# A hybrid streaming encoder layer: convolution sums moved to PSUM, part of the weight splitting moved to GpSimd

## The chip, the core and the metric

The kernel runs on one core of a Trainium2 chip. The metric is the device time of one execution in microseconds (us); the median of several runs is taken. TensorE (PE in the profile) does the matrix products, VectorE (DVE) and ScalarE (ACT) the work on elements, GpSimd (POOL) a few small copies, and SyncE (SP) issues all transfers.

## What is computed

One layer with three branches, fed by one projection of the normed input, for 512 prompt tokens and 64 sample tokens, 1024 channels wide (some steps left out):

```python
h = _rmsnorm(x, norm_pre_w)
proj = h @ w_in
glu_v, glu_g, conv_gate, z, xbc, dt_raw, q, xa_gate, gates = jnp.split(proj, points, axis=-1)

u = glu_v * jax.nn.sigmoid(glu_g)
c, new_a = _causal_dwconv(u, st_a, conv_dw_w, conv_dw_b)      # width 31
c = jax.nn.silu(_layernorm(c, conv_ln_w, conv_ln_b)) * jax.nn.silu(conv_gate)
out_a = c @ conv_out_w

xbc_c, new_ssd = _causal_dwconv(xbc, st_ssd, ssd_conv_w, ssd_conv_b)   # width 4
...                                       # state-space scan, gating, grouped norm
out_b = y.astype(x.dtype) @ ssd_out_w

s = jnp.einsum('bthd,bmhd->bhtm', qh, mem_k) * (XA_HEAD_DIM ** -0.5)
p = jax.nn.softmax(s, axis=-1)
o = jnp.einsum('bhtm,bmhd->bthd', p, mem_v)
out_c = (o * jax.nn.silu(xa_gate)) @ xa_out_w

g = jax.nn.sigmoid(gates + gate_b).reshape(bsz, t, N_BRANCH, D_MODEL)
m = g[:, :, 0] * out_a + g[:, :, 1] * out_b + g[:, :, 2] * out_c
x_new = x + _rmsnorm(m @ w_out, norm_post_w)
```

Cross-attention has 4 heads of 256 over 256 memory tokens. The long convolution, of width 31, is the one whose sums the change moves.

## The kernel before

**Tiling.** Channels lie on the 128 partitions and the 576 tokens along the free axis. Every projection is a job: one 1024 x 128 block of weights (or 512 x 256), loaded as a `raw` tile of 128 x 1024. Each float is split in two: ACT rounds it to a high part `whi` (L183), and the difference `raw - whi` is the low part `wlo` (L184, on DVE). The activations are split likewise (`hT[0]`, `hT[1]`, or `split`), and three products are summed for each of 8 blocks of rows: high by high, high by low, low by high (`mac`, L204). Two halves of 288 tokens make 48 matmuls for a whole projection. There are 153 jobs in a list `order`, and one of them ("dt") has no tile of its own for the low part; `prep_to` makes the parts of a job when the job two places ahead of it is asked for, and `raw`, `whi` and `wlo` have 3 buffers each.

**Stages.** First norm and transposes, then four groups of the state-space branch (to about 470 us in the profile) with their projections; in and after the last of them the gates of the long convolution (`glu(j)`, two projections gg and gv for each of the 8 channel blocks). Then the merge gate of the second branch (g1), the attention heads (for each head: key, query, key, query, two value jobs, two output gates xg; in heads 1 to 3 also a `glu`), the merges of the third branch (g2, oc), the gate cg of the convolution branch, its layer norm, and the merges of the first branch (g0, oa). At the end `out_rows` multiplies by w_out: four row blocks for each half of the channels, and `out_sample` after the second row block of the second half.

**The long convolution.** `conv_ops(j)` makes 32 operations for a channel block: a start value by ACT (L762: first tap and bias), 30 taps by DVE (L769: `c = u shifted * weight + c`, 606 columns), and the sum over blocks `csum` (L776, L778). They go in a list `bg`, and `bgrun(n)` puts n of them between the projections. `push_conv` takes two blocks at a time and lets them alternate: a tap of one, a tap of the other. The sums `c` lie in SBUF, a pool of 8 tiles (`c8`), from the first tap to the layer norm, which uses them as `cact[j]`.

**PSUM.** Two pools from start to end: `pmm` with 2 tiles of 2 x 512 columns for projections ("mm" in the profile), and `pps` with 4 tiles of 512 columns for everything else ("ps": transposes, key and value projections, attention scores, outputs of the heads, rows of the last product).

**Order.** The code states an order, but each engine's order is made when the kernel is built, `TileContext(nc, schedule_with_timeline_sim=True)`: an operation takes its place by its turn in the code, when its operands and a buffer are to be had. `keep_in_program_order` holds an operation (all taps, among others) to the order of the code, and `bgrun` runs with a lower turn. Once built, each engine works through its own list strictly in order.

**GpSimd's own work** after 376 us: for each `glu` a zero fill and a copy of the sample's state in `u` (L727, L728), and two small copies of the ends of `u` (L731, L732), which wait for DVE.

Of the kernel before, what the change touches and what calls it, by code (L numbers as in the profile page):

```python
# [8 lines left out]
F32 = mybir.dt.float32  # L9
F32R = mybir.dt.float32r  # L10
AF = mybir.ActivationFunctionType
ALU = mybir.AluOpType
# [16 lines left out]
def hybrid_trunk_kernel(  # L29
# [9 lines left out]
    nc = tc.nc  # L39
    PSUM = bass.MemoryType.PSUM  # L40
# [5 lines left out]
    wp = ctx.enter_context(tc.tile_pool(name="wp", bufs=2))  # L46
    big = ctx.enter_context(tc.tile_pool(name="big", bufs=1))
    pmm = ctx.enter_context(tc.tile_pool(name="pmm", bufs=2, space=PSUM))
    pps = ctx.enter_context(tc.tile_pool(name="pps", bufs=4, space=PSUM))
    dram = ctx.enter_context(tc.tile_pool(name="dram", bufs=1, space=bass.MemoryType.DRAM))  # L50

    def mm_tile():
        return pmm.tile([128, 2, 512], F32, tag="mm", name="mm")

    def ps_tile():
        return pps.tile([128, 512], F32, tag="ps", name="ps")


    ident = const.tile([128, 128], F32, name="ident")
# [102 lines left out]
    pos = {o[0]: i for i, o in enumerate(order)}  # L162
    ready = {}
    nprep = [0]

    def prep_to(n):
        while nprep[0] <= min(n, len(order) - 1):
            name, src, c0, r0, kk, cols = order[nprep[0]]
            raw = wp.tile([128, 1024], F32, tag="raw", name="raw", bufs=3)
            hi = wp.tile([128, 1024], F32R, tag="whi", name="whi", bufs=3)  # L170
            lo = wp.tile([128, 1024], F32R, tag="wlo", name="wlo", bufs=3) if name != "dt" else hi
            n_ = kk * cols
            nc.sync.dma_start(
                out=raw[:, :n_].rearrange("p (k c) -> p k c", k=kk),
                in_=src[r0:r0 + 128 * kk, c0:c0 + cols].rearrange("(k p) c -> p k c", p=128),
            )
            if name == "dt":
                w = hi[:, :2 * n_].rearrange("p (k c) -> p k c", k=kk)
                rw, wh, wl = raw[:, :n_].rearrange("p (k c) -> p k c", k=kk), w[:, :, 0:32], w[:, :, 32:64]
                a = nc.scalar.activation(wh, rw, AF.Copy)  # L180
                b = nc.vector.tensor_tensor(wl, rw, wh.bitcast(F32), ALU.subtract)
            else:
                a = nc.scalar.activation(hi[:, :n_], raw[:, :n_], AF.Copy)  # L183
                b = nc.vector.tensor_tensor(lo[:, :n_], raw[:, :n_], hi[:, :n_].bitcast(F32), ALU.subtract)  # L184
            if nprep[0] in (2, 3):
                tc.keep_in_program_order(a)
                tc.keep_in_program_order(b)
            ready[name] = (w, None) if name == "dt" else (
                hi[:, :n_].rearrange("p (k c) -> p k c", k=kk),
                lo[:, :n_].rearrange("p (k c) -> p k c", k=kk),  # L190
            )
            nprep[0] += 1

    def W(name):
        i = pos[name]
        prep_to(i + LA)
        return ready.pop(name)
# [46 lines left out]
    for t in range(5):  # L244
        n = 128 if t < 4 else 64
        if t < 4:
            x_t = obf[:, D * t:D * t + D]
        else:
            x_t = s2.tile([128, D], F32, tag="M", name="x4")
        nc.sync.dma_start(out=x_t[:n], in_=xp_d[128 * t:128 * t + 128] if t < 4 else xs_d)  # L250
        xt.append((x_t, n))
        if t == 0:
            wpre = s2.tile([128, D], F32, tag="R", name="wpre")
            nc.sync.dma_start(out=wpre, in_=norm_pre_w[0].partition_broadcast(128))
        if t == 1:
            prep_to(1)
# [11 lines left out]
    def x_tr(t):  # L268
        x_t, n = xt[t]
        rms_tile(x_t, n, sqx, ssx[:, t], wpre)  # L270
        for b in range(2):
            p = ps_tile()
            for k in range(4):
                kc = 512 * b + 128 * k
                m = nc.tensor.transpose(p[:, n * k:n * k + n], x_t[:n, kc:kc + 128], ident[:n, :n])
                tc.keep_in_program_order(m)
            v = p[:, :4 * n].rearrange("p (k t) -> p k t", k=4)
            d = slice(128 * t, 128 * t + n)
            nc.scalar.activation(hT[0][:, 4 * b:4 * b + 4, d], v, AF.Copy)
            nc.vector.tensor_tensor(  # L280
                hT[1][:, 4 * b:4 * b + 4, d], v, hT[0][:, 4 * b:4 * b + 4, d].bitcast(F32), ALU.subtract
            )

    def warm_pe(n):
        p = ps_tile()
        for _ in range(n):
            tc.keep_in_program_order(nc.tensor.matmul(p[:, 0:128], lhsT=ident, rhs=ident, start=True, stop=True))
# [27 lines left out]
    def tr_act(tiles, k, dst, wcol, ncols):  # L315
        pt = ps_tile()
        c = 0
        for x_t, n in tiles:
            nc.tensor.transpose(pt[:, c:c + n], x_t[:n, 128 * k:128 * k + 128], ident[:n, :n])
            c += n  # L320
        nc.scalar.activation(dst[0][:, k, :], pt[:, :ncols], AF.Copy, scale=vecs[:, wcol + k:wcol + k + 1])
        nc.vector.scalar_tensor_tensor(
            dst[1][:, k, :], pt[:, :ncols], vecs[:, wcol + k:wcol + k + 1],
            dst[0][:, k, :].bitcast(F32), ALU.mult, ALU.subtract,
        )
# [323 lines left out]
    def out_b(g, q):  # L649
        w = W(f"ob{g}_{q}")  # L650
        act = ([a for a, _ in yhl[g]], [b for _, b in yhl[g]])
        for i in range(2):
            m = 2 * q + i
            pt = proj(w, act=act, c0=128 * i)
            if g == 0:
                nc.scalar.activation(v2(ob[:, m]), va(pt), AF.Copy)
            else:
                nc.vector.tensor_tensor(v2(ob[:, m]), v2(ob[:, m]), va(pt), ALU.add)  # L658
# [13 lines left out]
    upad, cact = {}, {}  # L672
    bg = []
# [66 lines left out]
    for q in range(4):  # L740
        out_b(3, q)
    st.close()

    st = ExitStack()
    c8 = st.enter_context(tc.tile_pool(name="c8", bufs=8, reuse_waits="tile"))
    NC = 606
# [7 lines left out]
    def conv_ops(j):  # L754
        w31 = dww.rearrange("p (r j) -> p r j", r=31)
        box = []

        def first():
            c = c8.tile([128, NC], F32, tag="c", name="c")
            box.append(c)  # L760
            cact[j] = c
            nc.scalar.activation(  # L762
                c, upad[j][:, 0:NC], AF.Identity, scale=w31[:, 0, j:j + 1], bias=vecs[:, V_DWB + j:V_DWB + j + 1]
            )

        def tap(r):
            c = box[0]
            tc.keep_in_program_order(
                nc.vector.scalar_tensor_tensor(  # L769
                    c, upad[j][:, r:r + NC], w31[:, r, j:j + 1], c, ALU.mult, ALU.add  # L770
                )
            )

        def add():
            if j == 0:
                nc.vector.tensor_copy(csum, box[0])  # L776
            else:
                nc.vector.tensor_tensor(csum, csum, box[0], ALU.add)  # L778

        return [first] + [lambda r=r: tap(r) for r in range(1, 31)] + [add]  # L780

    def push_conv(*js):
        for ops in zip(*[conv_ops(j) for j in js]):
            bg.extend(ops)

    push_conv(0, 1)
    memT = [memp.tile([128, KD, NMEM], F32R, name=f"memT{i}") for i in range(2)]
    mt_ = []
# [6 lines left out]
    glu(3, sx, "xs", 7)  # L795
    glu(4, sx, "xs", 7)
    push_conv(2, 3)


# [90 lines left out]
    for h in range(4):  # L890
# [4 lines left out]
        cv = a1.tile([128, 2, 256], F32, tag="cv", name="cv")  # L895
# [20 lines left out]
        for tp in range(3):  # L916
            ps = ps_tile()
# [29 lines left out]
        for i in range(2):  # L947
            j = 2 * h + i
# [11 lines left out]
        if h > 0:  # L960
            glu(4 + h, sx, "xs", 7)
            if h != 2:
                push_conv(3 + h, 4 + h)
# [77 lines left out]
    for j in range(8):  # L1041
        c = cact[j]
# [111 lines left out]
    st3.close()  # L1154
    st.close()
    stx.close()


_INS = [
# [32 lines left out]
```

## Time and profile before

| | |
|---|---|
| median of 3 runs | 1123.3 us (1122.68 to 1123.66) |
| profiled execution | 1122.15 us |
| its span, first to last instruction | 1120.4 us |
| mean granted TensorE clock | 0.999 |
| GpSimd busy | 56.8 us in 146 instructions |
| long convolution's taps on DVE | 240, from 504.7 to 890.4 us |
| low parts on DVE | 152, from 10.7 to 1043.0 us |

How to read the rows: a row of the groups gives line, engine, operation, out<-in, shapes and count, then busy time and mean duration in ns, then the idle time of the engine before them and what ended it. A row of the timeline gives start, duration, engine, line, operation and count; rows of several instructions are merged. A row of the windows gives a stretch, and for PE, PEld, DVE, ACT, POOL the busy time and, in brackets, the instructions, then granted clock, share of the DMA engines and GB/s. A row of the waits gives who waited for whom, the total, the number and the longest. A row of the chain of waits gives start, duration and what ran. In the answer for one line, three numbers with slashes are the shortest, median and longest duration in ns.

### The profile page before, as it was taken

To read this page: it belongs to the slowest core of one execution; us is meant where nothing else is said; L and a number is where in the kernel's file an instruction comes from. 1 tells how busy PE (TensorE), PEld (TensorE's weight loads), DVE (VectorE), ACT (ScalarE), POOL (GpSimd) and SP (SyncE) were. 2 spreads that over 40 slices of the span, in tenths; PEclk is the share of its full clock that TensorE was granted. 3 is DMA by queue.
4 is the path that set the end of the run, shared out by engine and by line. 5 is a ranking of instruction groups with operands and counts; after the bars stand their busy time and mean duration, and the time that the engine had idled before them with its cause. 6 is when DMAs were issued, how large, how long until landed. Compare 5 with 4: busy or idle time off the path is not lost.

```text
span 1120.4 us, 20083 instructions
## 1 busy us (share of the span) xinstructions
PE 1109.5 (99%) x8285; PEld 1070.9 (96%) x8285; DVE 829.1 (74%) x1268; ACT 481.9 (43%) x844; POOL 56.8 (5%) x146
## 2 busy tenths in 40 slices
PE   8999999999999999999999999999999999999997
PEld 8999999999999999999999999999999999999974
DVE  5778897578868885756899996998588868714533
ACT  5564664456436442543224453434421245522331
POOL 0100110011002100100000000000000000000000
PEclk9999999999999999999999999999999999999999
DMA  7354423442353232242445343434353234233502
GB/s 208 95 162 122 143 82 94 129 117 81 97 144 107 83 81 78 75 124 76 135 139 142 85 131 95 123 85 116 84 160 93 76 84 106 76 94 104 178 20 85
DMA packets 183233, 120.74 MB, mean 108 GB/s; under 512 B 12422, under 2 KB 173230, under 8 KB 183142
## 3 DMA queue, kind: packets, MB, share of 16 engines
q1 hardware_dynamic: 183142, 119.46, 37.4%
q8 instruction: 65, 1.06, 0.4%
q14 instruction: 26, 0.21, 0.1%
HBM read 110.13 MB, written 9.31 MB: 107 GB/s over the span
## 4 chain that ended last, share of the span: by engine, by line
PE 97%; DMA 1%; ACT 1%; SPq 0%; DVE 0%; issue 0%; DVEq 0%; ACTq 0%
PE mm L204 78%; PE ps L204 4%; PE ps L887 2%; PE ps L886 2%; PE ps L888 2%; PE ps L561 2%; PE ps L587 2%; PE ps L565 1%; DMA ob<-in_x_prompt_dram 1%; PE ps L526 1%; PE ps L1130 1%; PE ps L518 1%; PE mm L346 0%; DMA out_dram<-ho 0%; PE ps L483 0%; PE ps L937 0%
## 5 line engine op out<-in xcount | busy, mean ns | idle before, releaser
L204 PE MATMUL mm<-hT,whi 128*128 128x288 f32 (+2 forms) x3328 | 588.3, 297 | 0.8 <-DVE hT L280 0.3
L204 PEld LDWEIGHTS mm<-hT,whi 128*128 128x128 f32 x3328 | 495.1, 189 | 3.6 <-issue 1.3
L204 PE MATMUL mm<-hT,wlo 128*128 128x288 f32 (+2 forms) x1664 | 363.9, 297 | 0.0
L183 ACT ACTIVATE whi<-raw 128x1024 fp32r<-128x1024 f32 x152 | 160.9, 1059 | 401.0 <-PE mm L204 323.9
L204 PEld LDWEIGHTS mm<-hT,wlo 128*128 128x128 f32 x1664 | 273.6, 189 | 1.1 <-issue 0.7
L184 DVE TENSOR_TENSOR wlo<-raw,whi 128x1024 fp32r<-128x1024 f32 x152 | 185.8, 1222 | 116.0 <-ACT whi L183 115.7
L769 DVE SCALAR_TENSOR_TENSOR c<-u,dww,c 128x606 f32<-128x606 f32 x240 | 191.5, 844 | 0.0
L204 PE MATMUL mm<-hi,whi 128*128 128x288 f32 x512 | 111.4, 298 | 0.0
L204 PE MATMUL mm<-lo,whi 128*128 128x288 f32 x512 | 110.9, 296 | 0.0
L204 PE MATMUL mm<-hi,wlo 128*128 128x288 f32 x512 | 110.4, 296 | 0.0
L204 PEld LDWEIGHTS mm<-hi,whi 128*128 128x128 f32 x512 | 82.2, 189 | 0.9 <-issue 0.9
L204 PEld LDWEIGHTS mm<-hi,wlo 128*128 128x128 f32 x512 | 82.5, 188 | 0.2 <-issue 0.2
L204 PEld LDWEIGHTS mm<-lo,whi 128*128 128x128 f32 x512 | 82.5, 188 | 0.0
L454 DVE SCALAR_TENSOR_TENSOR acc<-xp,scw,acc 128x579 f32<-128x579 f32 x72 | 58.4, 815 | 3.1 <-ACT acc L450 1.9
L658 DVE TENSOR_TENSOR ob<-ob,mm 128x576 f32<-128x576 f32 x24 | 18.0, 750 | 16.3 <-PE mm L204 16.2
L547 ACT ACTIVATE M<-R,tok 128x128 f32<-128x128 f32 (+1 forms) x80 | 24.8, 379 | 12.3 <-PE ps L587 12.3
L446 POOL COPY tails<-xp 128x3 f32<-128x3 f32 x24 | 18.0, 751 | 193.2 <-ACT xp L444 187.9
L887 PE MATMUL ps<-lo,hi 128*128 128x512 f32 x64 | 25.3, 397 | 0.0
L888 PE MATMUL ps<-hi,lo 128*128 128x512 f32 x64 | 25.1, 395 | 0.0
L886 PE MATMUL ps<-hi 128*128 128x512 f32 x64 | 24.9, 397 | 0.0
L565 PEld LDWEIGHTS ps<-bc,h 128*128 128x128 f32 x128 | 16.5, 191 | 8.8 <-issue 6.6
L204 PE MATMUL ps<-whi,memT 128*128 128x256 f32 x128 | 23.5, 282 | 0.0
(292 smaller groups left out, 1287.8 us busy)
## 6 DMA issues: line engine op xcount, KB each, us to landing
raw<-in_w_in_dram SPq DMA_DIRECT2D x104, 512.0 KB
R<-scr SPq DMA_DIRECT2D x16, 512.0 KB
raw<-in_ssd_out_w_dram SPq DMA_DIRECT2D x16, 512.0 KB
raw<-in_xa_kv_w_dram SPq DMA_DIRECT2D x16, 512.0 KB
raw<-in_xa_out_w_dram SPq DMA_DIRECT2D x8, 512.0 KB
raw<-in_conv_out_w_dram SPq DMA_DIRECT2D x8, 512.0 KB
wraw<-in_w_out_dram SPq DMA_DIRECT2D x8, 512.0 KB
E<-scr SPq DMA_DIRECT2D x24, 128.0 KB
```

Of the source, the lines that this page charges most:

```text
L183: a = nc.scalar.activation(hi[:, :n_], raw[:, :n_], AF.Copy)
L184: b = nc.vector.tensor_tensor(lo[:, :n_], raw[:, :n_], hi[:, :n_].bitcast(F32), ALU.subtract)
L204: m = nc.tensor.matmul(o, lhsT=w, rhs=r[:, s:s + w_], start=(i == 0 and a == 0), stop=(i == n - 1 and a == 2),)
L454: nc.vector.scalar_tensor_tensor(acc, xp[:, r:r + 579], w4[:, r, jt:jt + 1], acc, ALU.mult, ALU.add)
L547: nc.scalar.activation(M[:, 4 + e, :], R[:nl, 4 + e, :], AF.Relu, scale=-1.0, bias=tok[:nl, 0, c, a + 4:a + 5])
L561: nc.tensor.matmul(pS, lhsT=bt[:nl], rhs=xw[:nl], start=True, stop=True)
L565: nc.tensor.matmul(po[:, nl * j:nl * j + nl], lhsT=h[:, 128 * j:128 * j + 128], rhs=gC[g][:, cs], start=True, stop=True,)
L587: nc.tensor.matmul(pd[o:o + 64, nl * (e // 2):nl * (e // 2) + nl], lhsT=xd[:nl, 64 * e:64 * e + 64], rhs=M[:, e, :], start=True, stop=True,)
L769: nc.vector.scalar_tensor_tensor(c, upad[j][:, r:r + NC], w31[:, r, j:j + 1], c, ALU.mult, ALU.add)
L886: nc.tensor.matmul(out, lhsT=wh, rhs=rh, start=(i == 0), stop=False)
L887: nc.tensor.matmul(out, lhsT=wh, rhs=rl, start=False, stop=False)
L888: nc.tensor.matmul(out, lhsT=wl, rhs=rh, start=False, stop=(i == n - 1))
```

## The change

Three things. The convolution's sum is built in a PSUM tile of 1024 columns, of which 606 are used, in a pool with a single buffer; when a channel block is complete, ACT copies it to the SBUF tile that the layer norm uses, and DVE adds it to `csum` from PSUM. `push_conv` puts the blocks one after the other. To make room, the pool of 4 `ps` tiles is closed after the state-space branch and the last `out_b`, and a pool of 2 takes its place until the end. And for jobs behind `gv2` in the list, every second (odd place) has its low part made by GpSimd instead of DVE.

```diff
-    pps = ctx.enter_context(tc.tile_pool(name="pps", bufs=4, space=PSUM))
+    stp = ExitStack()
+    pps = stp.enter_context(tc.tile_pool(name="pps", bufs=4, space=PSUM))
...
+    psp = [pps]
+
     def ps_tile():
-        return pps.tile([128, 512], F32, tag="ps", name="ps")
+        return psp[0].tile([128, 512], F32, tag="ps", name="ps")
...
                 a = nc.scalar.activation(hi[:, :n_], raw[:, :n_], AF.Copy)
-                b = nc.vector.tensor_tensor(lo[:, :n_], raw[:, :n_], hi[:, :n_].bitcast(F32), ALU.subtract)
+                eng = nc.gpsimd if nprep[0] > pos["gv2"] and nprep[0] % 2 else nc.vector
+                b = eng.tensor_tensor(lo[:, :n_], raw[:, :n_], hi[:, :n_].bitcast(F32), ALU.subtract)
...
     st.close()
+    stp.close()
+    stp = ExitStack()
+    pcv = stp.enter_context(tc.tile_pool(name="pcv", bufs=1, space=PSUM))
+    psp[0] = stp.enter_context(tc.tile_pool(name="pps2", bufs=2, space=PSUM))
...
         def first():
-            c = c8.tile([128, NC], F32, tag="c", name="c")
+            c = pcv.tile([128, 1024], F32, tag="cv", name="cacc")[:, 0:NC]
             box.append(c)
-            cact[j] = c
...
         def add():
+            cact[j] = c8.tile([128, NC], F32, tag="c", name="c")
+            nc.scalar.activation(cact[j], box[0], AF.Copy)
             if j == 0:
                 nc.vector.tensor_copy(csum, box[0])
...
     def push_conv(*js):
-        for ops in zip(*[conv_ops(j) for j in js]):
-            bg.extend(ops)
+        for j in js:
+            bg.extend(conv_ops(j))
...
     stx.close()
+    stp.close()
```

## The prediction

> **What bounds the kernel now.** I read the page first, then the windows by stage, TensorE's own waits, and the timeline at the places that the change touches.
>
> ```profile
> span 1120.4 us, 20083 instructions
> ...
> PE 1109.5 (99%) x8285; PEld 1070.9 (96%) x8285; DVE 829.1 (74%) x1268; ACT 481.9 (43%) x844; POOL 56.8 (5%) x146
> ...
> DVE  5778897578868885756899996998588868714533
> ...
> PE 97%; DMA 1%; ACT 1%; SPq 0%; DVE 0%; issue 0%; DVEq 0%; ACTq 0%
> ```
>
> ```profile
> 0.00:15.00 15.00, 12.04 (x73) 11.25 (x73) 7.04 (x10) 9.69 (x18) 1.89 (x16) 1.00 0.95 271
> 15.00:476.00 461.00, 460.09 (x3554) 440.07 (x3555) 360.75 (x621) 241.08 (x458) 44.24 (x108) 1.00 0.37 106
> 476.00:1036.00 560.00, 560.00 (x4250) 556.92 (x4249) 425.02 (x582) 208.03 (x324) 10.66 (x22) 1.00 0.38 107
> 1036.00:1120.40 84.40, 77.35 (x412) 62.65 (x410) 36.28 (x59) 23.09 (x46) 0.00 (x0) 0.98 0.29 94
> ```
>
> TensorE (PE) is busy 1109.5 of 1120.4 us and is 97% of the chain that ended last. A busy PE could still be a slow one, so I check the rate and the waits.
>
> ```profile
> 655.00 12.80 PE mm L204 x96
> ```
>
> ```profile
> PE ps L287 <- POOL dtb L327: 1.6, 1, 1.6
> PE ps L1139 <- ACT ysq L1136: 0.8, 1, 0.8
> ```
>
> In the chain two whole projections of 48 matmuls take 12.80 us, 0.133 us for each of 288 columns, without a gap; the granted clock is 1.00 in that stage. The largest waits of PE are 1.6 us at the start and 0.8 us at the end. The change acts from the third gate projection on (about 476 us). From there to 1036 us PE is busy in all of the 560.00 us, while VectorE (DVE) has 560 - 425 = 135 us to spare and GpSimd (POOL) works for 10.7. So **a microsecond taken from DVE is worth nothing here, and a microsecond in which PE waits is added to the end.** What could be gained is the 7.05 us without PE work after 1036; most of it is the last row's evacuation and store, which the change leaves alone, and the rest is the 0.8 us above. A difference of 0.2%, 2.2 us, is about what a measurement of this kernel can tell from no change.
>
> **The change, part by part.**
>
> *Low parts on GpSimd.* After the third gate projection, jobs with an odd place in the list make their low part on GpSimd: 47 of 152 (counted in the list).
>
> ```profile
> L184 DVE TENSOR_TENSOR wlo<-raw,whi 128x1024 fp32r<-128x1024 f32 x152 | 185.8, 1222 | 116.0 <-ACT whi L183 115.7
> ...
> L769 DVE SCALAR_TENSOR_TENSOR c<-u,dww,c 128x606 f32<-128x606 f32 x240 | 191.5, 844 | 0.0
> ```
>
> DVE loses 47 x 1.222 = 57 us; none of it lies on PE's path: worth 0. What matters is whether a low part on GpSimd is late. The tightest of those 47 jobs that I found, the second key job of a head:
>
> ```profile
> 685.39 1.06 ACT L183 ACTIVATE whi<-raw 128x1024 fp32r<-128x1024 f32 x1 [8.19 <-PE mm L204]
> ```
>
> ```profile
> 694.69 0.40 PE L204 MATMUL ps<-memT,whi 128*128 128x256 f32 x2
> ```
>
> Its high part is ready at 686.45 and its first matmul runs at 694.69: 8.2 us of cover. (The second value job of a head has less, but its place is even and it stays on DVE.) No row shows a GpSimd operation of this size with two inputs.
>
> ```profile
> L237 POOL CAST onesr<-mask 128x128 fp32r<-128x128 f32 x1 | 0.3, 298 | 0.0
> ```
>
> ```profile
> L446 POOL COPY tails<-xp x24: 188/762/2412, 29.2 to 368.1; 128x3 f32<-128x3 f32 x24
> ```
>
> ```profile
> 136.20 1.22 DVE L184 TENSOR_TENSOR wlo<-raw,whi 128x1024 fp32r<-128x1024 f32 x1
> ```
>
> ```profile
> 136.27 1.20 POOL L446 COPY tails<-xp 128x3 f32<-128x3 f32 x1 [8.53 <-ACT xp L444]
> ```
>
> Bounds: below, DVE's own 1.22 us; above, the one-input cast of 128 columns times 8, and twice for two inputs, 4.8 us, plus the worst blocking: the tiny copy of L446 takes 0.19 us at best and 2.41 at worst, 2.2 more. That makes 7.0 us, still under 8.2. I take the cast times 8 and the copies' median blocking, 2.4 + 0.6 = 3.0 us. Cost on the path: 0, hidden by the two projections that run between a weight's making and its use. The raw buffer comes free up to 6 us later, and with it the next weight load on SP's queue and what stands behind it; the buffers run three jobs ahead, so 0 too. On POOL's own queue the low parts stand between the gates' small copies, which wait for DVE (L731 for L729); such a wait must also stay under 8.2 us.
>
> The row at 136.27 shows the copy ending with the DVE operation that has two SBUF inputs. The Trainium skill ("SBUF — State Buffer", Who interferes with whom) says that these two kinds block each other, the later one for the whole of the earlier. The trace agrees for GpSimd waiting; no row here shows DVE waiting, which is a rival below.
>
> *Sums in PSUM.* The 240 taps now read and write a PSUM tile. No row has a DVE write to PSUM; reading it costs nothing extra (L534 reads PSUM, L1050 does not, both 512 wide):
>
> ```profile
> L534 DVE TENSOR_TENSOR xd<-ps,tok 128x512 f32<-128x512 f32 x16 | 10.9, 680 | 0.0
> ...
> L1048 DVE SCALAR_TENSOR_TENSOR c<-th,c 128x606 f32<-128x606 f32 x8 | 6.0, 784 | 0.0
> ...
> L1050 DVE TENSOR_TENSOR hi<-hi,c 128x512 f32<-128x512 f32 x8 | 5.5, 685 | 0.0
> ...
> L1017 ACT ACTIVATE lsq<-c 128x606 f32<-128x606 f32 x7 | 4.9, 709 | 3.7 <-DVE csum L1018 3.7
> ```
>
> One tile at a time also means that each tap follows the one it depends on, where two channel blocks alternated before.
>
> ```profile
> 127.61 2.53 DVE L454 SCALAR_TENSOR_TENSOR acc<-xp,scw,acc 128x579 f32<-128x579 f32 x3
> ```
>
> ```profile
> 639.21 2.37 DVE L769 SCALAR_TENSOR_TENSOR c<-u,dww,c 128x606 f32<-128x606 f32 x3
> ```
>
> Three dependent operations of L454 (815 ns each) start (2.53 - 0.815)/2 = 0.857 us apart, 0.042 more than one lasts; three alternating taps (2.37 - 0.844)/2 = 0.763 apart, 0.081 less. So up to 0.12 us a tap, 240 x 0.12 = 29 us of DVE; in PSUM I take the same, with +-14 us as bounds (0.06 a tap, the gap between 844 and the 784 of L1048, a tap's width without the per-channel scalar). DVE still ends with 14 us or more fewer, inside its 135 spare: 0 on the path. Each block adds an ACT copy of 0.7 us (L1017's width); its tile is single, so between blocks the taps pause for that copy and the next start value, some 2 us seven times, with other DVE work to do. Cost: 0.
>
> *Half of the small PSUM tiles.* The new PSUM tile takes the room of two of the four [128, 512] tiles ("ps") from the opening of the new pools to the end. This is where PE can wait, and the only part that I give a price. In heads 1 to 3 three ps tiles are live when the value projection starts:
>
> ```profile
> 644.79 0.60 PE L860 MATMUL ps<-ident,kf 128*128 128x128 f32 x4
> 645.23 0.60 PE L911 MATMUL ps<-ident,ck 128*128 128x128 f32 x4
> 645.58 0.36 PE L204 MATMUL ps<-whi,memT 128*128 128x256 f32 x1
> ```
>
> ```profile
> 644.72 1.07 ACT L183 ACTIVATE whi<-raw 128x1024 fp32r<-128x1024 f32 x1 [1.93 <-PE mm L204]
> ...
> 646.22 0.59 ACT L862 ACTIVATE kk<-ps 128x512 f32<-128x512 f32 x1
> ```
>
> ```profile
> 645.86 1.22 DVE L184 TENSOR_TENSOR wlo<-raw,whi 128x1024 fp32r<-128x1024 f32 x1
> 647.00 0.75 DVE L904 TENSOR_TENSOR qlo<-mm,qhi 128x576 fp32r<-128x576 f32 x1
> ```
>
> With two, the matmul at 645.58 waits until ACT has copied the keys out, 646.22 + 0.59 = 646.81: 1.23 us. Head 3:
>
> ```profile
> 763.74 0.37 PE L204 MATMUL ps<-whi,memT 128*128 128x256 f32 x1
> ```
>
> ```profile
> 764.38 0.59 ACT L862 ACTIVATE kk<-ps 128x512 f32<-128x512 f32 x1
> ```
>
> Again 764.97 - 763.74 = 1.23; three heads 3.7 us. If PE fills each gap with the first four matmuls of the next projection, whose high part is ready at 645.79 (4 x 0.133 = 0.53; the fifth needs the low part), 2.1 remain. I take 2.1, bounds 0 and 3.7.
>
> Head 0 has no gate projections after it to fill with:
>
> ```profile
> 632.28 0.55 PE L956 MATMUL ps<-pts,cv 128*128 128x64 f32 x4
> 632.64 0.48 PE L204 MATMUL ps<-memT,whi 128*128 128x256 f32 x2
> ```
>
> ```profile
> 633.37 0.68 DVE L953 SCALAR_TENSOR_TENSOR oc<-ps,xs 128x512 f32<-128x512 f32 x1
> ...
> 634.72 0.68 DVE L953 SCALAR_TENSOR_TENSOR oc<-ps,xs 128x512 f32<-128x512 f32 x1
> ```
>
> Both tiles then hold results that DVE takes out until 634.05 and 635.40; the next key projection moves from 632.64 to 635.40, 2.8 us. If DVE comes to them earlier by a tap and a query split (0.84 + 0.75, the latter from L904) it is 1.2. I take 2.0. In the other heads 13 us of gate matmuls are there to fill: 0.
>
> At the end two tiles suffice for the rows, since one row is taken out while the next one's 24 matmuls run; only after the sample rows both tiles are held until DVE's L1137:
>
> ```profile
> 1102.50 0.69 DVE L1137 TENSOR_TENSOR y<-ps,x4r 128x512 f32<-128x512 f32 x1 [3.89 <-ACT ysq L1136]
> ```
>
> ```profile
> 1102.77 0.48 PE L886 MATMUL ps<-hi 128*128 128x512 f32 x1
> ```
>
> 1103.19 - 1102.77 = 0.4 us.
>
> **Sum:** 2.1 + 2.0 + 0.4 = 4.5 us. The profiled execution took 1122.15 us (span 1120.4), so 1126.65; it lies 1.15 under the median of the three runs, 1123.3, which gives **1127.8**.
>
> **The rivals.**
>
> *PE is refilled; no loss* (the other side: not slower). The order on PE is made anew and other matmuls move into each gap. Place: the value projections and head 0's end. For it: in the rows above PE already starts tiles out of the order of the code whenever one is missing, and never waits in 560 us. Against: at 645.58 the next projection's low part comes only at 647.08 (L184 at 645.86 + 1.22), and in the changed kernel GpSimd makes it (its place is odd). It decides from the point where each gap has more than 1.2 us of ready matmuls. Price 0: 1123.3, or 1122.5 with the 0.8 us wait gone too.
>
> *DVE blocked by GpSimd, tiles late.* If a GpSimd low part blocks DVE's operations as DVE blocked the copy at 136.27, a low part made by DVE waits up to 3.0 us, and behind it in DVE's order the maxima and the evacuations of ps (L871, L941, L953). With four tiles that was hidden; with two, one such delay in each head reaches PE: 4 x 3.0 = 12 us more, 1139.8. Against it: some 45 low parts, and those are spread over 550 us, so that most meet no such neighbour. By the Trainium skill's rule above, the taps, left with one tensor in SBUF, would not be blocked.
>
> *Low parts too late.* Over 8.2 us, each further microsecond costs 47 us: at 8.5, 1138 to 1142. It needs more than my upper bound of 7.0.
>
> *Faster by more than 2.2 us.* Nothing but shorter matmuls could do it, and none is touched.
>
> **How the numbers follow.** Forecast (1125.6 to 1131) 0.45; refilled 0.34; DVE blocked 0.14; low parts too late 0.03; faster 0.04. All unknowns at their lower ends give 1122.5, all PE waits at their upper ends 3.7 + 2.8 + 0.4 = 6.9, 1130.2. Range 1122.4 to 1137: it leaves out the faster case and the upper half of the blocked one, and what lies past it. Both signs of cases hold much of the chance, so the likeliest one's own range, 1125.6 to 1131, stands beside it. Faster 0.04; same 0.35; slower 0.61.
>
> **What would show it.** Right: PE busy falls short of the stage 476 to 1036 by some 4 us, TensorE's waits list ACT L862 and DVE L953, DVE is down 15 to 60 us, and the end moves by what PE waits. Wrong: PE gains waits on GpSimd's L184 (low parts late), or on DVE operations that last 2 us or more (blocking), or none at all (refilled). A change in the matmuls' 0.133 us would void the whole argument.

## The result and the profile after

| | before | after |
|---|---|---|
| median | 1122.99 us (4 runs, 1122.50 to 1123.66) | 1131.72 us (4 runs, 1130.24 to 1132.12) |
| ratio, 95% interval | | 1.0075 [1.0057, 1.0092] |
| profiled execution | 1122.15 us | 1132.04 us |

The changed kernel is slower by 8.7 us, 0.75%. First the page of the kernel after: the span, the busy times, and from the costliest groups the taps and the low parts made by GpSimd.

```profile
span 1130.3 us, 20124 instructions
...
PE 1112.8 (98%) x8285; PEld 1071.7 (95%) x8285; DVE 825.4 (73%) x1221; ACT 487.4 (43%) x852; POOL 168.5 (15%) x193
...
L776 DVE SCALAR_TENSOR_TENSOR cacc<-u,dww,cacc 128x606 f32<-128x606 f32 x240 | 203.9, 850 | 9.8 <-ACT cacc L769 4.9
...
L188 POOL TENSOR_TENSOR wlo<-raw,whi 128x1024 fp32r<-128x1024 f32 x47 | 116.5, 2479 | 412.0 <-ACT whi L186 310.3
```

DVE lost 47 low parts of 1.22 us, 57 us, and yet is busy only 3.7 us less (829.1 to 825.4). Something gave nearly all of it back. The window of the kernel after for the stage used before (columns as there):

```profile
476.00:1036.00 560.00, 554.96 (x4183) 549.52 (x4183) 418.63 (x532) 210.44 (x328) 116.45 (x67) 1.00 0.37 104
```

Where PE was busy in all of 560 us it now lacks 5.04. Of TensorE's waits in the kernel after, these three are new behind 476 us:

```profile
PE mm L208 <- DVE hi L468: 3.2, 1, 3.2
PE ps L208 <- ACT kk L871: 1.7, 4, 1.0
...
PE ps L895 <- ACT sss L1149: 0.4, 1, 0.4
```

There is one of 3.2 us for the evacuation of a gate cg (`hi`, the product after the tanh, L464 before and L468 now), four for the copy of the keys `kk`, and 0.4 at the tail. The largest was not in the forecast's sum. Here is its place, the layer norm, in the timeline of the kernel after:

```profile
938.45 2.40 POOL L188 TENSOR_TENSOR wlo<-raw,whi 128x1024 fp32r<-128x1024 f32 x1 [9.86 <-ACT whi L186]
...
939.06 7.33 DVE L1052 TENSOR_TENSOR c<-c,mean 128x606 f32<-128x606 f32 x8
...
946.32 0.74 DVE L468 SCALAR_TENSOR_TENSOR hi<-hi,mm 128x576 f32<-128x576 f32 x1
...
947.12 0.80 PE L208 MATMUL mm<-hT,whi 128*128 128x288 f32 x4 [3.17 <-DVE hi L468]
...
948.14 1.17 PE L208 MATMUL mm<-hT,whi 128*128 128x288 f32 x4
...
949.58 1.17 PE L208 MATMUL mm<-hT,whi 128*128 128x288 f32 x4
```

and the same place in the timeline of the kernel before:

```profile
936.00 0.74 DVE L464 SCALAR_TENSOR_TENSOR hi<-hi,mm 128x576 f32<-128x576 f32 x1
936.65 5.68 DVE L1043 TENSOR_TENSOR c<-c,mean 128x606 f32<-128x606 f32 x8
...
944.40 0.75 DVE L464 SCALAR_TENSOR_TENSOR hi<-hi,mm 128x576 f32<-128x576 f32 x1
```

The reader is to see three things. The eight products with the tile `mean` (which by then holds the reciprocal deviation) take 7.33 us in place of 5.68, and they begin while GpSimd makes a low part; one of them lasts 2.43 us and the other seven 0.77. The evacuation that PE needs stands behind these eight in DVE's list; before, one stood ahead of them. And after the wait PE comes back slowly: from 948.14 to 949.58 it starts six matmuls (two lie between the rows), one in 0.24 us where 0.133 was the rule. The window behind the wait, of the kernel after, shows how long (the column before the last two is the granted clock):

```profile
947.00:951.00 4.00, 3.88 (x18) 3.89 (x19) 4.00 (x7) 0.33 (x1) 0.00 (x0) 0.61 0.37 85
951.00:955.00 4.00, 4.00 (x31) 4.00 (x31) 4.00 (x9) 2.50 (x4) 0.00 (x0) 0.97 0.39 116
```

The clock lacks 0.39 of 4 us and 0.03 of 4 us, 1.7 us together, as half a clock for 3.4 us would give. In 3.4 us at 0.24 a matmul PE starts 14 of them, which would have taken 1.9: 1.5 us is lost on top of the 3.2. In this execution one evacuation that came late cost 4.7 us; what the clock adds differs from one execution to the next, as the last section shows.

Which operations of DVE got longer is in its groups, kernel after and then kernel before (count | busy us, mean ns of one | idle before):

```profile
L1001 DVE TENSOR_TENSOR ob<-ob,xs 128x576 f32<-128x576 f32 x8 | 15.3, 1918 | 0.1
...
L1021 DVE TENSOR_TENSOR c<-c,mean 128x606 f32<-128x606 f32 x8 | 7.9, 1050 | 0.0
...
L1052 DVE TENSOR_TENSOR c<-c,mean 128x606 f32<-128x606 f32 x8 | 7.3, 982 | 0.0
```

```profile
L992 DVE TENSOR_TENSOR ob<-ob,xs 128x576 f32<-128x576 f32 x8 | 6.0, 753 | 0.0
...
L1012 DVE TENSOR_TENSOR c<-c,mean 128x606 f32<-128x606 f32 x8 | 5.7, 783 | 0.0
L1043 DVE TENSOR_TENSOR c<-c,mean 128x606 f32<-128x606 f32 x8 | 5.7, 784 | 0.0
```

All of these read two tensors in SBUF. The taps, which now read one in SBUF and one in PSUM, keep their time (844 to 850). So the first theory was that **GpSimd's low parts stop DVE where it reads two SBUF tensors**, which costs nothing in most places and some 5 us at the layer norm; the two `ps` tiles cost the rest. Against it stood two rivals: that the sums, now complete later (the last tap starts at 895.51 and not at about 890.4), push the layer norm into the gates; and that the two tiles upset everything.

### The profile page after: what moved, and what is told of

Same layout as the page of the kernel before. It is cut to its first block, busy times and chain, and to the rows that moved or that the text cites. A ratio compares the mean times of both kernels' runs of the same rounds, so it can differ in the third digit from the quotient of the medians.

```text
span 1130.3 us, 20124 instructions
## 1 busy us (share of the span) xinstructions
PE 1112.8 (98%) x8285; PEld 1071.7 (95%) x8285; DVE 825.4 (73%) x1221; ACT 487.4 (43%) x852; POOL 168.5 (15%) x193
## 5 line engine op out<-in xcount | busy, mean ns | idle before, releaser
L776 DVE SCALAR_TENSOR_TENSOR cacc<-u,dww,cacc 128x606 f32<-128x606 f32 x240 | 203.9, 850 | 9.8 <-ACT cacc L769 4.9
L188 DVE TENSOR_TENSOR wlo<-raw,whi 128x1024 fp32r<-128x1024 f32 x105 | 128.1, 1220 | 95.3 <-ACT whi L186 94.7
L188 POOL TENSOR_TENSOR wlo<-raw,whi 128x1024 fp32r<-128x1024 f32 x47 | 116.5, 2479 | 412.0 <-ACT whi L186 310.3
L1000 DVE SCALAR_TENSOR_TENSOR lo<-lo,mm 128x576 f32<-128x576 f32 x8 | 6.0, 754 | 27.1 <-PE mm L208 27.1
```

The source lines that it names most:

```text
L188: b = eng.tensor_tensor(lo[:, :n_], raw[:, :n_], hi[:, :n_].bitcast(F32), ALU.subtract)
L776: nc.vector.scalar_tensor_tensor(c, upad[j][:, r:r + NC], w31[:, r, j:j + 1], c, ALU.mult, ALU.add)
```

## The experiments

Each kernel was timed together with the kernel before. The table gives medians and the ratio to the kernel before; 0.1% is 1.1 us. "Sums" says where the convolution's sum is built.

| kernel | low parts on GpSimd | sums | ps tiles | median us | ratio [95%] |
|---|---|---|---|---|---|
| the change | 47 | PSUM | 2 | 1131.72 | 1.0075 [1.0057, 1.0092] |
| e1 | 47 | SBUF | 4 | 1141.42 | 1.0159 [1.0146, 1.0173] |
| e2 | none | PSUM | 2 | 1126.23 | 1.0034 [1.0021, 1.0046] |
| e3 | none | SBUF | 2 | 1127.30 | 1.0039 [1.0027, 1.0052] |
| e4 | 42, none at the norm | PSUM | 2 | 1126.23 | 1.0029 [1.0018, 1.0041] |
| e5 | 47, mean in PSUM | PSUM | 2 | 1127.60 | 1.0041 [1.0028, 1.0053] |
| e6 | 5, at the norm only | SBUF | 4 | 1128.48 | 1.0046 [1.0032, 1.0060] |
| e7 | none | SBUF, one tile at a time | 4 | 1123.00 | 1.0003 [0.9994, 1.0012] |
| e8 | 42, none at the norm | SBUF | 4 | 1135.62 | 1.0111 [1.0097, 1.0124] |
| e9 | 42, none at the norm | PSUM | 2, values in mm | 1123.20 | 1.0005 [0.9997, 1.0014] |
| e10 | none | SBUF | 2, values in mm | 1123.02 | 1.0004 [0.9995, 1.0013] |

### e1: the low parts on GpSimd alone

On the kernel before:

```diff
-                b = nc.vector.tensor_tensor(lo[:, :n_], raw[:, :n_], hi[:, :n_].bitcast(F32), ALU.subtract)
+                eng = nc.gpsimd if nprep[0] > pos["gv2"] and nprep[0] % 2 else nc.vector
+                b = eng.tensor_tensor(lo[:, :n_], raw[:, :n_], hi[:, :n_].bitcast(F32), ALU.subtract)
```

> The kernel before, with only the 47 low parts on GpSimd: four ps tiles, sums in SBUF, two blocks alternating. Theory 'DVE blocked at the layer norm': the low parts on GpSimd stretch DVE's additions and products with two SBUF inputs (0.70 us each before) to 2 us and more where both run, the evacuation of a gate cg comes late, and TensorE loses some 5 us there (3.2 of wait, 1.7 of a halved clock). This kernel then shows nearly all of that: 1123.0 + 5 = 1128, with PE waits on the evacuation of mm and none on the keys' copy kk. Rival 'the sums are late': the later last tap of the sums moves the layer norm; this kernel keeps the old sums, so 1123.0 and no new wait of PE. Rival 'two small tiles': also 1123.0.

Measured: 1141.42 us, 18.6 over the kernel before, over twice the whole change. Every theory missed this; the sign of the first was right and its size far too small. TensorE's waits in e1:

```profile
PE ps L889 <- DVE qlo L905: 3.3, 3, 2.1
PE mm L205 <- DVE hi L465: 3.2, 1, 3.2
PE ps L888 <- DVE ptl L942: 2.4, 2, 1.2
PE ps L205 <- DVE memT L323: 1.6, 1, 1.6
```

The 3.2 us at the layer norm is there, as expected. New are waits in the heads, for the low parts of queries and probabilities, and one for the transposed memory. The three timelines of e1 at the longest of them, of DVE, of GpSimd and of TensorE:

```profile
774.33 6.02 DVE L770 SCALAR_TENSOR_TENSOR c<-u,dww,c 128x606 f32<-128x606 f32 x5
...
780.97 0.74 DVE L905 TENSOR_TENSOR qlo<-mm,qhi 128x576 fp32r<-128x576 f32 x1
```

```profile
773.51 3.14 POOL L185 TENSOR_TENSOR wlo<-raw,whi 128x1024 fp32r<-128x1024 f32 x1 [6.45 <-PE ps L912]
```

```profile
781.77 0.58 PE L889 MATMUL ps<-khi,qlo 128*128 128x256 f32 x1 [2.08 <-DVE qlo L905]
```

Five taps take 6.02 us where five took 3.9 at the alternating taps' pace of 0.763 us; the first began while GpSimd's low part ran. With the sums in SBUF a tap reads two SBUF tensors, and the taps are what DVE does most in the heads. One tap in e1 lasted 2994 ns, and the mean rose from 844 to 1034 ns:

```profile
L770 DVE SCALAR_TENSOR_TENSOR c<-u,dww,c x240: 818/839/2994, 486.1 to 903.8; 128x606 f32<-128x606 f32 x120
```

So the two halves of the change belong together: the sums in PSUM shield the taps from GpSimd. The runs that follow test this too.

### e2 and e3: the sums in PSUM alone, two tiles alone

e2 is the changed kernel with `nc.vector` again for every low part; e3 is the kernel before with the second pool only:

```diff
+    stp.close()
+    stp = ExitStack()
+    psp[0] = stp.enter_context(tc.tile_pool(name="pps2", bufs=2, space=PSUM))
```

> The changed kernel with every low part back on DVE: sums in PSUM one at a time, two ps tiles. Theory 'DVE blocked at the layer norm': what is left is the wait for the keys' copy in four heads (2.9 us between starts of matmuls in the changed kernel) and 0.4 at the tail: 1123.0 + 3.3 = 1126.3; no operation of the layer norm on DVE lasts over 0.8 us. Rival 'the sums are late': the loss of 5 us at the layer norm stays, 1131.7, and PE waits for the evacuation of a gate cg. Rival 'two small tiles': 1131.7 too.

> The kernel before with two ps tiles from the third gate group's end on and nothing else: sums in SBUF and alternating, low parts on DVE. Theory 'DVE blocked': 2.9 us at the value projections of the heads and 0.4 at the tail, 1126.3, as for the sums in PSUM. Rival 'two small tiles': all of the change, 1131.7. Rival 'the sums are late': 1126.3 too, since the sums are the old ones; it is told from the first theory by the kernel with the PSUM sums alone.

Measured: 1126.23 and 1127.30, ratios 1.0034 and 1.0039 with intervals that overlap; both lost about what the first theory gives to two tiles. TensorE's waits in e2 that are new, beside the 0.4 us at the tail:

```profile
PE mm L207 <- ACT whi L186: 1.0, 2, 0.8
PE ps L207 <- ACT kk L870: 0.9, 4, 0.2
```

The second is the wait for the keys' copy; the first is PE at the fill, a projection begun before its high part is there. None is for a gate's evacuation, though in e2 the last tap starts at 902.3 us, later than in the change. So "the sums are late" is out. "Two small tiles make all of it" is out as well.

### e4: the five low parts at the layer norm on DVE

On the changed kernel:

```diff
-                eng = nc.gpsimd if nprep[0] > pos["gv2"] and nprep[0] % 2 else nc.vector
+                ln = pos["cg0"] <= nprep[0] <= pos["g0_0"]
+                eng = nc.gpsimd if nprep[0] > pos["gv2"] and nprep[0] % 2 and not ln else nc.vector
```

> The changed kernel, but the five low parts that fall into the layer norm (jobs cg0 to g0_0) are made by DVE; the other 42 stay on GpSimd. Theory 'DVE blocked at the layer norm': the 5.1 us there go, although DVE has 5 x 1.22 us more to do: 1131.7 - 5 = 1126.6, and no halved clock at 947 us. Rival 'the sums are late' or 'two small tiles': 1131.7 or more, since DVE gets more work at the place where it is late.

Measured: 1126.23 us; ratio 1.0029 against 1.0075, so 5.2 us of the 8.7 hang on five instructions, although DVE has 6.1 us more to do there. The timeline of DVE in e4:

```profile
939.08 0.74 DVE L469 SCALAR_TENSOR_TENSOR hi<-hi,mm 128x576 f32<-128x576 f32 x1
939.74 5.68 DVE L1053 TENSOR_TENSOR c<-c,mean 128x606 f32<-128x606 f32 x8
```

The eight take 5.68 us again, and the evacuation stands ahead of them again. That the order changed back with the durations leaves a question: was it the blocking or the order? e5 answers it. The other 42 low parts on GpSimd cost nothing that can be measured: e4 and e2 have the same median, though their ratios are each known only to some 0.12%.

### e5: the mean in PSUM

The changed kernel, all 47 low parts on GpSimd; only the second operand of the sixteen operations of the layer norm moves, into the tile that the sums have left:

```diff
-    mean = e2.tile([128, NC], F32, tag="npw", name="mean", bufs=1)
...
     bgrun(10000)
+    mean = pcv.tile([128, 1024], F32, tag="cv", name="mean")[:, 0:NC]
     ln_mean()
```

> The changed kernel with all its 47 low parts on GpSimd; only the tile 'mean' of the layer norm (mean, then reciprocal deviation) lies in PSUM, in the tile that the sums have left, so that c - mean and c * mean (16 operations) read one SBUF tensor instead of two. Theory 'DVE is blocked only where it reads two SBUF tensors': both groups of eight take 5.7 us again, as before the change, instead of 7.9 and 7.3, and the 5.1 us at the layer norm go at least for the most part: 1126 to 1128. Rival 'GpSimd slows any DVE operation', or 'the order of the layer norm is what is late': 1131.7 and the wait for the gate's evacuation stays.

Measured: 1127.60 us, ratio 1.0041. The groups of DVE in e5:

```profile
L1026 DVE TENSOR_TENSOR csum<-csum,lsq 128x606 f32<-128x606 f32 x7 | 7.2, 1030 | 1.9 <-ACT lsq L1025 1.6
...
L1020 DVE TENSOR_TENSOR c<-c,mean 128x606 f32<-128x606 f32 x8 | 5.7, 779 | 0.0
L1052 DVE TENSOR_TENSOR c<-c,mean 128x606 f32<-128x606 f32 x8 | 5.7, 779 | 0.0
```

The sixteen with one operand in PSUM are free of GpSimd (779 ns each); the sums of squares, which still read two SBUF tensors, are not (1030 against 788 before). In this kernel the evacuation still stands behind the eight, as in the change (timeline of DVE in e5):

```profile
937.84 5.66 DVE L1052 TENSOR_TENSOR c<-c,mean 128x606 f32<-128x606 f32 x8
943.41 0.75 DVE L468 SCALAR_TENSOR_TENSOR hi<-hi,mm 128x576 f32<-128x576 f32 x1
```

The wait is there and is short, and the granted clock behind it is 1.00 (the mean from 920 to 960 us). TensorE's waits in e5:

```profile
PE mm L208 <- DVE hi L468: 0.8, 1, 0.8
```

So the blocking of the operations with the mean makes most of the loss: in the profiled executions 3.2 us of wait and 1.5 at the clock become 0.8. The 0.8 that stays goes with the order that was built, the evacuation behind the eight; whether the sums of squares, which are still blocked, have a part in it is not shown. The Trainium skill ("SBUF — State Buffer", Who interferes with whom) says that a DVE instruction with at most one SBUF input, outside its two-port modes, does not contend with GpSimd. e5 and the change agree, at 779 against 1050 ns, and so do the taps, at 850 ns in the change against 1034 in e1.

### e6 and e8: five low parts alone, and the other 42 alone

Both on the kernel before, with sums in SBUF and four tiles; e6 has `nprep[0] % 2 and ln` as its condition, e8 the condition of e4.

> The kernel before, with only the five low parts of jobs cg0 to g0_0 on GpSimd: sums in SBUF, four ps tiles, the 147 other low parts on DVE. Theory 'DVE blocked at the layer norm': these five are enough, 1123.0 + 5 = 1128, with a PE wait of 2 to 3 us for a gate cg's evacuation and a halved clock behind it. Rival 'it takes the later sums or the small tiles too': 1123.0 to 1124, blocked operations but no wait of PE.

> The kernel before with 42 low parts on GpSimd, the five at the layer norm on DVE: sums in SBUF, four ps tiles. Theory 'the taps need the PSUM sums as a shield': with sums in SBUF each tap reads two SBUF tensors and is blocked; of the 18.6 us that all 47 cost alone, the 5.1 of the layer norm go, so about 1123 + 13 = 1136, PE waits on DVE's qlo and ptl, taps of up to 3 us. Rival 'what all 47 cost alone comes from the layer norm or from the order that was made': 1123 to 1126.

Measured: e6 1128.48 us, ratio 1.0046, that is 5.2 us from five instructions, and the same wait as in the change. TensorE's waits in e6:

```profile
PE mm L206 <- DVE hi L466: 3.2, 1, 3.2
```

Its five executions run from 1126.70 us, at a mean granted clock of 0.999, to 1130.62, at 0.995, so the 5.2 is the middle of a spread that goes with the clock.

e8: 1135.62 us, ratio 1.0111. The same 42 low parts that cost nothing with the sums in PSUM (e4 against e2) cost 12.5 us with the sums in SBUF. The order of the blocks and the number of ps tiles differ between these pairs too, but the taps tell for the shield: beside the 42 low parts their mean is 1035 ns in e8 and 850 in e4. e6 and e8 together give 1.57%, e1 has 1.59%.

### e7: one block after the other, in SBUF

```diff
-        for ops in zip(*[conv_ops(j) for j in js]):
-            bg.extend(ops)
+        for j in js:
+            bg.extend(conv_ops(j))
```

> The kernel before with the blocks of the long convolution one after the other, sums in SBUF: each tap depends on the one before it. By the prediction up to 0.12 us more a tap, 29 us of DVE at most, all beside TensorE: 1123.0, no new wait of PE. Rival 'dependent taps delay the evacuations behind them': 1125 or more, with PE waits on DVE in the heads.

Measured: 1123.00 us, no difference; DVE's busy time rises from 829.1 to 841.1 us. Of the 53 us that DVE got back from somewhere in the change (57 less 3.7), these 12 go with the order of the taps. Of the other 41, eleven kinds of operation that read two SBUF tensors account for 36 in the groups of the two kernels (9.3 for `ob` and 3.8 for the mean in the groups above); besides them, the taps and the low parts, no kind differs by more than 0.3, and some 5 us are not assigned. Dependent taps are slower, as forecast; a row each of the timelines of e7 and of the change:

```profile
564.91 3.50 DVE L769 SCALAR_TENSOR_TENSOR c<-u,dww,c 128x606 f32<-128x606 f32 x4
```

```profile
565.67 4.40 DVE L776 SCALAR_TENSOR_TENSOR cacc<-u,dww,cacc 128x606 f32<-128x606 f32 x5
```

(3.50 - 0.85)/3 = 0.88 us from start to start in SBUF and (4.40 - 0.85)/4 = 0.89 in PSUM, against 0.763 for alternating blocks: 0.12 a tap, which comes from the dependence and not from PSUM, and is hidden.

### e9 and e10: the values out of the ps tiles

On e4 and on e3, one line in `v_proj`:

```diff
-        pv = ps_tile()
+        pv = mm_tile()[:, 0]
```

> The kernel with the five low parts of the layer norm back on DVE (1126.2), and the value projection of the four heads in half of an mm tile in place of a ps tile. Theory 'what is left is the wait of the value projection for a third ps tile': the waits for the keys' copy kk go, 2.9 us, and only the tail's 0.4 stays: 1123.3. Rival 'the mm tile is then missing instead': the two mm tiles hold a query and the values until ACT has copied them, and the gate projections wait about as long: 1126 or more, with PE waits of mm matmuls on ACT.

> The kernel before with two ps tiles (1127.3), and the value projection in half of an mm tile. Theory 'third ps tile': 1127.3 - 2.9 and what else the heads lose there, 1123.4 to 1124.4. Rival 'the mm tile is then missing instead': 1127 or more.

Measured: 1123.20 and 1123.02 us, ratios 1.0005 and 1.0004; neither can be told from the kernel before. So the third live `ps` tile was the whole price of the smaller pool that can be measured, and an mm tile is free at that moment. e9 keeps the sums in PSUM and 42 low parts on GpSimd and costs nothing. It gains nothing either: no experiment pointed to a version that is faster than the kernel before, and none of them shortens what PE does.

## Why the prediction was right in sign and too small

It said slower, by 4.5 us; it was 8.7 us, inside the range and above the forecast's own one (1125.6 to 1131). That it lies in the range owes something to luck: of the sum's 4.5 us, 2.0 were not lost at all, and the largest loss, 5.2 us, stands in no term of it. The range reached so far up for the sake of a rival that had the mechanism and the wrong place. DVE's busy time, which was to fall by 15 to 60 us, fell by 3.7. Step by step:

- **What bounds the kernel.** Right. DVE is busy 843.0 us in e2 and 823.1 in e4, and the two have the same median; the losses that were found are waits of PE, the matmuls cut off before them, and the clock behind them.
- **"What matters is whether a low part on GpSimd is late": this is the step that failed.** None was late; no wait of PE names them, and the answer for their line in the kernel after (shortest, median and longest in ns) has 2.40 us for the estimated 3.0:

```profile
L188 POOL TENSOR_TENSOR wlo<-raw,whi x47: 2372/2403/2992, 464.5 to 1045.8; 128x1024 fp32r<-128x1024 f32 x47
```

What mattered is whom they stop. The mechanism was written down as the rival "DVE blocked by GpSimd, tiles late", with a chance of 0.14, and placed at the heads' `ps` evacuations, 3.0 us in each. In the change that place costs nothing (e4 against e2); the place is the layer norm, where eight operations in a row read two SBUF tensors and a gate's evacuation stands behind them. It cost 5.2 us, at one place (e4, e6). The sum went by DVE's spare 135 us over the whole stage. In the layer norm itself there was hardly any, as this window of the kernel before shows (DVE, the third busy time, works in 36.03 of 40 us):

```profile
920.00:960.00 40.00, 40.00 (x306) 39.93 (x305) 36.03 (x50) 24.16 (x32) 0.00 (x0) 1.00 0.36 95
```

- **Sums in PSUM, price 0.** Right (e2 is no slower than e3), with the 0.12 us a tap confirmed where taps follow one another; the 29 us of DVE that this was to make came to 12 (e7). The remark that taps with one tensor in SBUF would not be blocked was right, and weighs more than the text gave it: without that shield the 42 low parts outside the norm cost 12.5 us.
- **The value projections, 2.1 us (0 to 3.7) in heads 1 to 3.** Right in mechanism, too large for these three heads, and head 0 was left out. e9 against e4 gives 2.7 for all four (the ratios' difference, 0.24%, with some 1.6 us of noise either way). PE fills with four matmuls, as forecast. Of the four waits the longest, 1.01, is in head 0; the other three share 0.7, 0.23 each. The timeline of the kernel after there:

```profile
600.41 0.79 PE L208 MATMUL mm<-hT,whi 128*128 128x288 f32 x4
600.80 0.85 ACT L769 ACTIVATE cacc<-u,vecs,dww 128x606 f32<-128x606 f32 x1
...
601.58 0.59 ACT L871 ACTIVATE kk<-ps 128x512 f32<-128x512 f32 x1
...
602.22 0.38 PE L208 MATMUL ps<-whi,memT 128*128 128x256 f32 x1 [1.01 <-ACT kk L871]
```

The start value of the next channel block (0.85 us on ACT), which the prediction costed at nothing, stands ahead of the keys' copy, and the difference between the heads is 0.78. The list of waits says 1.7 in all, less than what is lost: the four matmuls at 600.41 take 0.79 us until they end, 0.26 over 4 x 0.133, and PE loses this too at each break. Four times 0.26 and 1.7 make 2.7, of which 0.5 falls to each of heads 1 to 3 and 1.3 to head 0.

- **Head 0's end, 2.0 us.** Wrong: the change loses nothing there (in e3 PE waits 0.62 us at this place, for a high part). The order on PE was made anew: the next query projection runs ahead of the key projection that has no tile. DVE and PE in the timelines of the kernel after:

```profile
632.61 0.69 DVE L962 SCALAR_TENSOR_TENSOR oc<-ps,xs 128x512 f32<-128x512 f32 x1 [0.45 <-PE ps L897]
...
635.90 0.68 DVE L962 SCALAR_TENSOR_TENSOR oc<-ps,xs 128x512 f32<-128x512 f32 x1
```

```profile
635.31 0.70 PE L208 MATMUL mm<-hT,whi 128*128 128x288 f32 x4
...
639.45 0.41 PE L208 MATMUL ps<-memT,whi 128*128 128x256 f32 x2
```

The rival "PE is refilled" held at this place; at the value projections it held only in part.

- **The tail, 0.4 us.** Right: 0.4 in TensorE's waits.

The parts: 5.2 for the layer norm (e4 or e6), 2.7 for the heads, 0.4 at the tail make 8.3 of 8.7. The profiled pair differs by 9.9 us; part of that lies in the first 80 us, which the change does not touch, and runs of one kernel differ by some 2 us as well.

## What to carry to other kernels

Before work is moved to GpSimd, list the DVE operations that read two tensors in SBUF and look at what stands behind them in DVE's list, stage by stage; an average of free DVE time says nothing about the one stage in which DVE is nearly full. Putting one of the two operands in PSUM takes such an operation out of GpSimd's way, which can be worth more than the operation itself. When a pool of tiles is halved, count the live tiles at each point; here one tile too few at one point was the whole price, and another pool had it free.

## What the runs showed of the hardware that was not expected

**A short wait of PE has a second price.** After a wait of 3.17 us (the change) and one of 2.08 (e1, at 781.77) the granted clock fell; after waits of 1.6 us and less (e1, e5) it did not. In the change it lacked 1.7 us of full clock, as computed above. e1's window at its wait shows a granted clock of 0.91 over 20 us, so 1.8 us:

```profile
770.00:790.00 20.00, 17.91 (x134) 17.71 (x133) 17.95 (x26) 9.51 (x22) 5.67 (x2) 0.91 0.48 134
```

The Trainium skill ("TensorE: Matmul & The Clock Gate", Part 1: The HAM clock gate) says that the array runs at half its clock after at least one idle window of about 3.4 us and at full clock after at least one busy window of that length, and that the windows run freely. The half clock and the length agree here: 1.7 and 1.8 are half of 3.4 and 3.6. But waits of 2.1 and 3.2 us, shorter than such a window, were enough.

The second price is not fixed. After the same wait of 3.17 us, e1 and e6 lost twice as much at the clock as the change: their granted clock is 0.72 in the 12 us from 952 (e1) and from 940 (e6), so it lacks 3.4 us, the half clock for 6.8. e6's profiled execution is also the slowest of its five. What decides between one length and two, these runs do not show.

**The blocking goes both ways.** GpSimd's low part takes 2.40 us at the median and up to 2.99 in the change; its mean rises from 2479 ns (the change) to 2935 in e1, where the taps read two SBUF tensors. A tap of 0.84 us that meets one lasts up to 2.99 us in e1. The rows of the layer norm fit a wait for all that is left of GpSimd's operation: the eight products began at 939.06 with 1.79 of its 2.40 us to go, and took 1.65 us longer than before.
